# SSD decay sums through DRAM: a store and broadcast loads in place of ones-matmuls, and the head matmuls in one chain

## The chip, the core and the metric

One NeuronCore of a Trainium2 chip runs the whole program: TensorE (PE, with its weight loads shown as PEld), VectorE (DVE), ScalarE (ACT), GpSimd (POOL), SyncE (SP, which only issues transfers) and 16 DMA engines behind the queues of SP, ACT and POOL. The metric is device time in microseconds for one execution, the median of the runs shown. All arithmetic is float32; where a projection needs speed, an operand is split into a high and a low part in the faster format fp32r.

## What is computed

Two layers of a decoder over 256 positions and 2048 features. The change lies in layer 0, in its SSD mixer (32 heads of 64 channels, four groups of state size 128, one chunk of 256 positions):

```python
z, xbc, dt, q, k, v, gate = split(x @ w_in)
xs, bm, cm = split(silu(causal_depthwise_conv(xbc)))
dt = softplus(dt + dt_bias);  a = dt * -exp(a_log)      # per position and head
a_cum = cumsum(a)                                       # along the 256 positions
decay[l, s] = exp(a_cum[l] - a_cum[s])  for s <= l, else 0
y[l] = sum_s (cm[l] . bm[s]) * decay[l, s] * dt[s] * xs[s]  +  d_skip * xs[l]
y_a = rms_norm(y * silu(z))
```

Beside it, on the same input, runs an attention branch with 16 heads (q, k, v, gate). Both outputs go through one projection, a residual and a LayerNorm, and then layer 1 follows (a diagonal state-space mixer), which the change does not touch.

## The kernel before

The big projections set the frame. Each weight matrix comes in **units** of 512 KB: `split_to` loads one on SP's queue into a tile `raw` (four buffers), ACT copies it to a high part `wh`, and DVE subtracts to a low part `wl` (four buffers each). TensorE multiplies a unit while the next three are being prepared: `xmm` (L293) has 12 matmuls of 512 columns for a unit, and `product_wide` (L348, L349) 16 for a unit. So TensorE always has projection matmuls, and everything else is fitted in between.

That everything else is written as small **jobs**. After each unit, `pump` takes some of two queues: `jobs`, which has to be done by the end of the running projection, and `back`, which is spread evenly up to the unit `goal`. `run` puts the instructions of a job behind the load and the split of the unit two ahead, on each engine's queue. Beyond that, a scheduler that simulates the program in time orders each engine's instructions at build: among the ready ones it prefers those that were written earlier. `tc.issue_after(ins)` adds one rule to it: what is written inside and runs on the engine of `ins` is queued behind `ins`; it is an order, not a wait.

For SSD, `dt_jobs` computes dt and the cumulative sums for all 32 heads with heads on partitions: `r`, [32, 256]. `turn` (L559) transposes them into `dts` and `cums`, with positions on partitions, so that each position s has its scalar. The decay also needs the sums along the free axis, the same row on all 128 partitions. For that, `r` is split into a high and a low part in `cumhl` (L556, L557, rows 0 to 31 and 32 to 63, rest zero), and `sel` holds a unit vector for each head.

`head_jobs(k)` handles the two heads 2k and 2k+1, for k from 0 to 15, in steps:

- `bcast` (L842): for each head a matmul with one column of `sel` repeated 128 times as weights and `cumhl` as moving operand. It leaves the head's sums on all partitions in a PSUM tile of the pool `aux`.
- `decay` (L848 to L850): ACT computes relu(cums - row) for two halves of each head, out of PSUM into the tile `df` (tag b3, four buffers, shared with the rotary and attention tiles), then exp of the negative.
- `weigh` (L855 to L860): DVE multiplies with dt and the masked products of B and C (`cbm`), and adds the skip weight on the diagonal.
- `apply` (L872, L873): the product with the head's channels. A head's output has 64 rows, so head i of a pair writes partitions 64 i to 64 i + 63 and uses half of the array's columns. Its first matmul has 256 columns, its second 128, summed in PSUM; each float32 matmul shows as two records. An even and an odd k share one PSUM tile, and their applies are due in one step: a **couple** of four heads, eight couples in all.
- `comb` (L877 to L881): gate, square and sum, for the couple.

`skewed` lays these steps over one another: in background step t, apply belongs to k = t - 3 (and t - 4), weigh to t - 2, decay to t - 1, bcast to t. There are 20 steps; `goal` gives them the 48 units of the rest of the z projection and of q, k and v of the first attention group. The rotary jobs of q and k, which also use b3, run during the last 16 of these units.

Of the kernel before, what the change touches and what calls it, by code (L numbers as in the profile page):

```python
# [9 lines left out]
F32 = mybir.dt.float32  # L10
F32R = mybir.dt.float32r
AF = mybir.ActivationFunctionType
OP = mybir.AluOpType
# [3 lines left out]
P = 128  # L17
S = 256
# [3 lines left out]
CU = KT // UK  # L22
# [148 lines left out]
def trunk(tc, io, out):  # L171
# [8 lines left out]
    with ExitStack() as top:  # L180
# [10 lines left out]
        def C(name):  # L191
            lo, hi = CONST[name]
            return ct[:, lo:hi]

        def PR(name):
            lo, hi = PARAM[name]
            return pt[:, lo:hi]
# [3 lines left out]
        def aux():  # L201
            return auxp.tile([P, 512], F32, tag="aux", name=nm("aux"))
# [252 lines left out]
        with ExitStack() as l0:  # L455
# [6 lines left out]
            def b3(shape):  # L462
                return wk.tile(shape, F32, tag="b3", bufs=4, name=nm("b3"))
# [40 lines left out]
                    T.matmul(pdt, wdp[:, k, :], xh[:, k, :], start=k == 0, stop=False, skip_group_check=True)  # L504
                    T.matmul(pdt[:32], wdp[:, k, 0:32], xl[:, k, :], start=False, stop=k == KT - 1, skip_group_check=True)

            cumhl = wk.tile([P, S], F32R, name="cumhl")
            sel = cst.tile([P, 32], F32R, name="sel")
            G.memset(cumhl[64:128, :].bitcast(F32), 0.0)
            dts = wk.tile([P, 2, 32], F32, name="dts")  # L510
            cums = wk.tile([P, 2, 32], F32, name="cums")

            def dt_jobs():
                h = {}

                def soft1():
                    A.activation(sel, C("sel"), AF.Copy)
                    dw = wk.tile([32, 4, S], F32, tag="a4", bufs=6, name="dw")
                    ew = wk.tile([32, 4, S], F32, tag="a4", bufs=6, name="ew")
                    h["d"] = [dw[:, i, :] for i in range(4)]  # L520
                    h["e"] = [ew[:, i, :] for i in range(4)]
                    sx, na, e, r = h["d"]
                    A.activation(na, hdt["p"][32:64, :], AF.Copy)
                    V.scalar_tensor_tensor(sx, hdt["p"][0:32, :], PR("dtb")[:32, :], na, op0=OP.add, op1=OP.add)
                    V.scalar_tensor_tensor(na, sx, -1.0, sx, op0=OP.mult, op1=OP.min)
                    A.activation(e, na, AF.Exp)
                    V.tensor_scalar(r, e, 2.0, None, op0=OP.add)
                    V.reciprocal(r, r)

                def soft2():  # L530
                    sx, na, e, r = h["d"]
                    u, w2, pl, dtv = h["e"]
                    G.tensor_tensor(u, e, r, op=OP.mult)
                    G.tensor_tensor(w2, u, u, op=OP.mult)
                    G.tensor_scalar(pl, w2, 1.0 / 17, None, op0=OP.mult)
                    for k in range(7, 4, -1):
                        G.tensor_scalar(pl, pl, 1.0 / (2 * k + 1), None, op0=OP.add)
                        G.tensor_tensor(pl, pl, w2, op=OP.mult)

                def soft3():  # L540
                    u, w2, pl, dtv = h["e"]
                    for k in range(4, -1, -1):
                        G.tensor_scalar(pl, pl, 1.0 / (2 * k + 1), None, op0=OP.add)
                        G.tensor_tensor(pl, pl, w2 if k else u, op=OP.mult)

                def soft4():
                    sx, na, e, r = h["d"]
                    u, w2, pl, dtv = h["e"]
                    V.tensor_scalar(sx, sx, 0.0, None, op0=OP.max)
                    V.scalar_tensor_tensor(dtv, pl, 2.0, sx, op0=OP.mult, op1=OP.add)  # L550
                    ea = wk.tile([32, 1], F32, name="ea")
                    A.activation(ea, PR("alog")[:32, :], AF.Exp)
                    V.tensor_scalar(na, dtv, ea, -1.0, op0=OP.mult, op1=OP.mult)
                    V.memset(e, 1.0)
                    V.tensor_tensor_scan(r, e, na, 0.0, op0=OP.mult, op1=OP.add)
                    A.activation(cumhl[0:32, :], r, AF.Copy)  # L556
                    V.tensor_tensor(cumhl[32:64, :], r, cumhl[0:32, :].bitcast(F32), op=OP.subtract)  # L557

                def turn():  # L559
                    sx, na, e, r = h["d"]  # L560
                    u, w2, pl, dtv = h["e"]
                    px = aux()
                    for t in range(2):
                        T.transpose(px[:, t * 32 : t * 32 + 32], dtv[:, t * P : t * P + P], ident[:32, :32])
                        T.transpose(px[:, 64 + t * 32 : 96 + t * 32], r[:, t * P : t * P + P], ident[:32, :32])
                    A.activation(dts.rearrange("p t h -> p (t h)"), px[:, 0:64], AF.Copy)
                    A.activation(cums.rearrange("p t h -> p (t h)"), px[:, 64:128], AF.Copy)

                return [soft1, soft2, soft3, soft4, turn]
# [261 lines left out]
            G.memset(ssq, 0.0)  # L831
            G.memset(ones, 1.0)

            def head_jobs(k):
                d = {}
                g = k // 4
                heads = [(i, 2 * k + i) for i in range(2)]

                def bcast():
                    d["px"] = aux()  # L840
                    for i, h in heads:
                        T.matmul(d["px"][:, i * 256 : i * 256 + 256], sel[:, h : h + 1].to_broadcast([P, P]), cumhl, start=True, stop=True)  # L842

                def decay():
                    df = d["df"] = b3([P, 2, 384])
                    for i, h in heads:
                        pc = d["px"][:, i * 256 : i * 256 + 256]
                        A.activation(df[:, i, 0:256], pc, AF.Relu, bias=cums[:, 0, h : h + 1], scale=-1.0)  # L848
                        A.activation(df[:, i, 256:384], pc[:, 128:256], AF.Relu, bias=cums[:, 1, h : h + 1], scale=-1.0)
                    A.activation(df, df, AF.Exp, scale=-1.0)  # L850

                def weigh():
                    df = d["df"]
                    for i, h in heads:
                        V.scalar_tensor_tensor(df[:, i, 0:256], df[:, i, 0:256], dts[:, 0, h : h + 1], cbm[:, g, 0:256],  # L855
                                               op0=OP.mult, op1=OP.mult)
                        V.scalar_tensor_tensor(df[:, i, 256:384], df[:, i, 256:384], dts[:, 1, h : h + 1], cbm[:, g, 256:384],
                                               op0=OP.mult, op1=OP.mult)
                        dg = df[:, i, :].rearrange("p (b n) -> p b n", b=3)[:, 0:3:2, :]
                        V.scalar_tensor_tensor(dg, ident.unsqueeze(1).to_broadcast([P, 2, P]), PR("ssdd")[:, h : h + 1], dg,  # L860
                                               op0=OP.mult, op1=OP.add)

                def apply():
                    if k % 2 == 0:
                        pairy[0] = aux()
                    y = d["y"] = pairy[0]
                    df = d["df"]
                    yp = y[:, (k % 2) * S : (k % 2) * S + S]
                    for i, h in heads:
                        xc = slice(64 * h, 64 * h + 64)  # L870
                        yo = yp[64 * i : 64 * i + 64, :]
                        T.matmul(yo, xs[:, 0, xc], df[:, i, 0:256], start=True, stop=False)  # L872
                        T.matmul(yo[:, 128:256], xs[:, 1, xc], df[:, i, 256:384], start=False, stop=True)  # L873

                def comb():
                    sv = sz[:, k - 1 : k + 1, :].rearrange("p f n -> p (f n)")
                    V.tensor_tensor(sv, d["y"], sv, op=OP.mult)  # L877
                    jk = c2([P, 2, S])
                    A.activation(jk.rearrange("p f n -> p (f n)"), sv, AF.Square)  # L879
                    for f in range(2):  # L880
                        G.tensor_tensor(ssq, ssq, jk[:, f, :], op=OP.add)  # L881

                return [bcast, decay, weigh, apply, comb] if k % 2 else [bcast, decay, weigh, lambda: None, apply]

            pairy = [None]

            def skewed(lists):
                n = max(len(x) for x in lists)
# [19 lines left out]
            for j in range(4):  # L908
                zs = sz[:, 4 * j : 4 * j + 4, :]
                product_wide(xhl, lambda zs=zs: zs, lambda h, zs=zs: jobs.append(lambda: A.activation(zs, zs, AF.Silu)) if h else None)  # L910
                if j == 0:
                    jobs.extend(held)
                    goal[0] = unit[0] + 6 * CU
                    back.extend(skewed([head_jobs(k) for k in range(16)]))

            yb = {}
# [618 lines left out]
```

## Time and profile before

| | us |
|---|---|
| median of 3 runs | 1332.26 |
| lowest, highest | 1331.92, 1332.73 |
| profiled execution, its own time | 1332.87 |
| its span, first to last instruction | 1331.0 |
| mean granted TensorE clock | 0.999 |

The profile gives each engine's busy time, the chain of work that ended last, and groups of instructions by line with what ended the idle time before them. A line such as `L842 PE MATMUL aux<-cumhl,sel 128*128 128x256 f32 x32 | 7.4, 307 | 0.0` reads: line 842, engine, operation, what it writes and reads, its form, the count, then busy us, mean ns of one, and idle us before. Matmuls overlap, so their lengths do not add up; the order in time has start and length of each in microseconds from the start of the span.

### The profile page before, as it was taken

How to read it: one execution, taken by the hardware profiler on the slowest of the kernel's cores; microseconds unless marked ns; L12 is line 12 of the kernel's file. 1: busy time of each engine (PE TensorE's matmuls, PEld its weight loads, DVE VectorE, ACT ScalarE, POOL GpSimd, SP SyncE). 2: the span in 40 equal slices, each digit the busy share in tenths (PEclk: the TensorE clock that was granted, in tenths of full speed). 3: DMA queues.
4: the chain of work that ended last, by engine and by line, in shares of the span. 5: the costliest groups of instructions: out<-in, count | busy, mean ns of one | idle time of the engine just before them, and what ended most of it. 6: DMA issues, size and time to landing. Idle time of an engine off the chain costs nothing.

```text
span 1331.0 us, 21530 instructions
## 1 busy us (share of the span) xinstructions
PE 1321.8 (99%) x8079; PEld 1111.5 (84%) x8079; DVE 961.6 (72%) x1612; ACT 692.8 (52%) x947; POOL 337.9 (25%) x646
## 2 busy tenths in 40 slices
PE   9999999999999999999999999999999999999998
PEld 8988888877888888888888888888888888888886
DVE  6778877775686777687797765858999846555565
ACT  5556668864644554554564434443445544444442
POOL 0043000121036625334787300023453100000000
PEclk9999999999999999999999999999999999999999
DMA  8555555444556657656757768469998675555762
GB/s 318 175 183 181 180 175 174 155 149 157 173 190 225 196 204 234 201 189 202 235 189 247 253 230 308 173 232 308 321 292 303 216 215 188 190 190 190 252 211 90
DMA packets 80732, 282.73 MB, mean 212 GB/s; under 512 B 9842, under 2 KB 12658, under 8 KB 80116
## 3 DMA queue, kind: packets, MB, share of 16 engines
q1 hardware_dynamic: 68260, 239.64, 54.4%
q0 software_dynamic: 7328, 30.42, 6.8%
q10 hardware_dynamic: 5040, 11.31, 2.4%
q8 instruction: 63, 1.03, 0.3%
q14 instruction: 41, 0.34, 0.1%
HBM read 260.35 MB, written 20.97 MB: 211 GB/s over the span
## 4 chain that ended last, share of the span: by engine, by line
PE 97%; DMA 2%; DVE 0%; ACT 0%; issue 0%; SPq 0%; ACTq 0%; POOLq 0%
PE main L293 61%; PE main L348 16%; PE main L349 8%; PE main L315 3%; PE aux L429 2%; DMA ud<-ut 1%; PE aux L872 1%; PE aux L780 1%; DMA um<-ud 1%; PE dec L1335 1%; PE aux L961 1%; PE enc L1290 1%; PE aux L993 1%; PE dec L1331 0%; PE aux L790 0%; PE aux L842 0%
## 5 line engine op out<-in xcount | busy, mean ns | idle before, releaser
L249 DVE TENSOR_TENSOR wl<-raw,wh 128x1024 fp32r<-128x1024 f32 x430 | 533.1, 1242 | 306.5 <-ACT wh L244 304.4
L244 ACT ACTIVATE wh<-raw 128x1024 fp32r<-128x1024 f32 x430 | 455.2, 1060 | 518.4 <-PE main L293 313.4
L293 PE MATMUL main<-wh,A 128*128 128x512 f32 x1536 | 490.0, 394 | 0.0
L293 PEld LDWEIGHTS main<-wh,A 128*128 128x128 f32 x1536 | 287.8, 188 | 59.2 <-issue 0.3
L293 PE MATMUL main<-wl,A 128*128 128x512 f32 x768 | 300.7, 392 | 0.0
L348 PE MATMUL main<-A,wh 128*128 128x512 f32 x768 | 273.1, 399 | 0.0
L293 PE MATMUL main<-wh,C 128*128 128x512 f32 x832 | 262.4, 393 | 0.3 <-ACT C L1110 0.3
L349 PE MATMUL main<-A,wl 128*128 128x256 f32 x768 | 215.3, 280 | 0.0
L293 PEld LDWEIGHTS main<-wh,C 128*128 128x128 f32 x832 | 155.6, 188 | 34.0 <-ACT C L1110 1.0
L348 PEld LDWEIGHTS main<-A,wh 128*128 128x128 f32 x768 | 144.2, 188 | 33.6
L293 PEld LDWEIGHTS main<-wl,A 128*128 128x128 f32 x768 | 144.3, 188 | 29.2 <-issue 0.5
L293 PE MATMUL main<-wl,C 128*128 128x512 f32 x416 | 162.5, 391 | 0.0
L349 PEld LDWEIGHTS main<-A,wl 128*128 128x128 f32 x768 | 145.1, 189 | 0.2
L706 POOL TENSOR_TENSOR c<-c 128x8 f32<-128x8 f32 (+2 forms) x192 | 97.3, 525 | 28.6 <-DMA wb<-c 21.0
L293 PEld LDWEIGHTS main<-wl,C 128*128 128x128 f32 x416 | 78.1, 188 | 16.2
L348 PE MATMUL main<-C,wh 128*128 128x512 f32 x192 | 68.2, 399 | 0.0
L934 POOL TENSOR_TENSOR b<-b 128x128 f32<-128x128 f32 x16 | 11.4, 710 | 194.5 <-DVE b L933 151.6
L881 POOL TENSOR_TENSOR ssq<-ssq,c 128x256 f32<-128x256 f32 x16 | 18.4, 1147 | 166.4 <-ACT c L879 165.9
L349 PE MATMUL main<-C,wl 128*128 128x256 f32 x192 | 53.6, 281 | 0.0
L708 POOL TENSOR_TENSOR c<-c,c 128x4 f32<-128x4 f32 (+2 forms) x96 | 46.5, 485 | 7.4
L709 POOL TENSOR_TENSOR c<-c,c 128x4 f32<-128x4 f32 (+2 forms) x96 | 45.7, 476 | 0.0
L315 PE MATMUL main<-A,wh 128*128 128x256 f32 x256 | 43.4, 284 | 1.4 <-ACT wh L236 1.4
(302 smaller groups left out, 1379.2 us busy)
## 6 DMA issues: line engine op xcount, KB each, us to landing
raw<-in_wi SPq DMA_DIRECT2D x270, 512.0 KB, 3.7
raw<-in_wo SPq DMA_DIRECT2D x96, 512.0 KB, 4.3
raw<-in_wglu SPq DMA_DIRECT2D x64, 512.0 KB, 3.3
wt<-wb POOLq DMA_DIRECT2D x16, 896.0 KB, 7.4
wb<-ob ACTq DMA_DIRECT2D x16, 512.0 KB, 5.1
bc<-in_s5bc SPq DMA_DIRECT2D x16, 256.0 KB, 3.8
wb<-c POOLq DMA_DIRECT2D x16, 256.0 KB, 3.8
wb<-om ACTq DMA_DIRECT2D x16, 128.0 KB, 3.3
```

What stands on the lines that cost most here:

```text
L244: high = A.activation(wh, raw, AF.Copy)
L249: splits[n] = (loaded[-1], high, V.tensor_tensor(wl, raw, wh.bitcast(F32), op=OP.subtract))
L293: end = T.matmul(ps[o], l[:, k, sl], r[:, j, :], start=start and i == 0, stop=stop and i == 2)
L315: T.matmul(pv[o // 2][:, o % 2, :], l[:, j, sl], r[:, k, :], start=first and i == 0 and o % 2 == 0, stop=end and i == 2 and o % 2 == 1, sk ...
L348: T.matmul(ps[o], wh[:, j, sl], xx[:, k, :, :].rearrange("p a n -> p (a n)"), start=first, stop=False, skip_group_check=True)
L349: T.matmul(ps[o][:, S : 2 * S], wl[:, j, sl], xh[:, k, :], start=False, stop=end, skip_group_check=True)
L429: end = T.transpose(dst[:, i * P : i * P + P], s, ident)
L706: G.tensor_tensor(p[:, :, :, 0:m], cs[:, :, :, 1 : m + 1], cs[:, i, :, n : n + 1].unsqueeze(1).to_broadcast([P, 2, 4, m]), op=OP.mult)
L708: G.tensor_tensor(cs[:, 0, :, n + 1 : n + 1 + m], p0[:, 0, :, 0:m], p1[:, 1, :, 0:m], op=OP.subtract)
L709: G.tensor_tensor(cs[:, 1, :, n + 1 : n + 1 + m], p0[:, 1, :, 0:m], p1[:, 0, :, 0:m], op=OP.add)
L780: T.matmul(pk[at : at + 64, 64 * n + a * 16 : 64 * n + a * 16 + 16], d["ev"][:, a, 64 * i : 64 * i + 64], cv[:, a, i, :], start=True, stop ...
L881: G.tensor_tensor(ssq, ssq, jk[:, f, :], op=OP.add)
```

## The change

The cumulative sums `r` are written to a tile `cumd` in DRAM by a DMA on POOL's queue, in place of the high and low parts; `cumhl`, `sel` and their filling are gone. A new first step `spread` takes the place of `bcast`: it allocates `df` and loads the two heads' rows on SP's queue into it, each repeated over all 128 partitions. `decay` reads them there and works in place, the second half first. `apply` is now one function of the odd k, for both k of the couple: it gives out the four heads' matmuls in turns (odd k first), each queued behind the one before. `goal` becomes three units smaller.

```diff
-            cumhl = wk.tile([P, S], F32R, name="cumhl")
-            sel = cst.tile([P, 32], F32R, name="sel")
-            G.memset(cumhl[64:128, :].bitcast(F32), 0.0)
+            cumd = dram.tile([32, S], F32, name="cumd")
...
-                    A.activation(sel, C("sel"), AF.Copy)
...
-                    A.activation(cumhl[0:32, :], r, AF.Copy)
-                    V.tensor_tensor(cumhl[32:64, :], r, cumhl[0:32, :].bitcast(F32), op=OP.subtract)
+                    nc.gpsimd.dma_start(cumd, r)
...
+            couple = {}
+
             def head_jobs(k):
-                d = {}
+                d = couple[k % 2] = {}
+                pair = (couple.get(0), d)
...
-                def bcast():
-                    d["px"] = aux()
+                def spread():
+                    d["df"] = b3([P, 2, 384])
+                    nc.sync.dma_start(d["df"][:, :, 0:256], cumd.rearrange("(k i) n -> k i n", i=2)[k : k + 1].to_broadcast([P, 2, S]))
+
+                def decay():
+                    df = d["df"]
                     for i, h in heads:
-                        T.matmul(d["px"][:, i * 256 : i * 256 + 256], sel[:, h : h + 1].to_broadcast([P, P]), cumhl, start=True, stop=True)
-
-                def decay():
-                    df = d["df"] = b3([P, 2, 384])
-                    for i, h in heads:
-                        pc = d["px"][:, i * 256 : i * 256 + 256]
-                        A.activation(df[:, i, 0:256], pc, AF.Relu, bias=cums[:, 0, h : h + 1], scale=-1.0)
-                        A.activation(df[:, i, 256:384], pc[:, 128:256], AF.Relu, bias=cums[:, 1, h : h + 1], scale=-1.0)
+                        A.activation(df[:, i, 256:384], df[:, i, 128:256], AF.Relu, bias=cums[:, 1, h : h + 1], scale=-1.0)
+                        A.activation(df[:, i, 0:256], df[:, i, 0:256], AF.Relu, bias=cums[:, 0, h : h + 1], scale=-1.0)
                     A.activation(df, df, AF.Exp, scale=-1.0)
...
-                        V.scalar_tensor_tensor(dg, ident.unsqueeze(1).to_broadcast([P, 2, P]), PR("ssdd")[:, h : h + 1], dg,
-                                               op0=OP.mult, op1=OP.add)
+                        d["w"] = V.scalar_tensor_tensor(dg, ident.unsqueeze(1).to_broadcast([P, 2, P]), PR("ssdd")[:, h : h + 1], dg,
+                                                        op0=OP.mult, op1=OP.add)

                 def apply():
-                    if k % 2 == 0:
-                        pairy[0] = aux()
-                    y = d["y"] = pairy[0]
-                    df = d["df"]
-                    yp = y[:, (k % 2) * S : (k % 2) * S + S]
-                    for i, h in heads:
-                        xc = slice(64 * h, 64 * h + 64)
-                        yo = yp[64 * i : 64 * i + 64, :]
-                        T.matmul(yo, xs[:, 0, xc], df[:, i, 0:256], start=True, stop=False)
-                        T.matmul(yo[:, 128:256], xs[:, 1, xc], df[:, i, 256:384], start=False, stop=True)
+                    y = d["y"] = aux()
+                    ahead = d["w"]
+                    for n, e in ((1, pair[1]), (0, pair[0])):
+                        for part in range(2):
+                            for i in range(2):
+                                h = 2 * (k - 1 + n) + i
+                                yo = y[64 * i : 64 * i + 64, n * S : n * S + S]
+                                xc = slice(64 * h, 64 * h + 64)
+                                with tc.issue_after(ahead.ins):
+                                    if part:
+                                        ahead = T.matmul(yo[:, 128:256], xs[:, 1, xc], e["df"][:, i, 256:384], start=False, stop=True)
+                                    else:
+                                        ahead = T.matmul(yo, xs[:, 0, xc], e["df"][:, i, 0:256], start=True, stop=False)
...
-                return [bcast, decay, weigh, apply, comb] if k % 2 else [bcast, decay, weigh, lambda: None, apply]
-
-            pairy = [None]
+                return [spread, decay, weigh, apply, comb] if k % 2 else [spread, decay, weigh]
...
-                    goal[0] = unit[0] + 6 * CU
+                    goal[0] = unit[0] + 6 * CU - 3
```

## The prediction

> **What bounds the kernel now.** I read the page first, then the busy time of the stretch in which the changed work lies, then single instructions of TensorE in order of time, then the groups and the waits of the engines that feed it.
>
> ```profile
> span 1331.0 us, 21530 instructions
> ...
> PE 1321.8 (99%) x8079; PEld 1111.5 (84%) x8079; DVE 961.6 (72%) x1612; ACT 692.8 (52%) x947; POOL 337.9 (25%) x646
> ...
> PE 97%; DMA 2%; DVE 0%; ACT 0%; issue 0%; SPq 0%; ACTq 0%; POOLq 0%
> ```
>
> ```profile
> 184.00:330.00 146.00, 146.00 (x802) 119.92 (x801) 103.27 (x172) 102.95 (x164) 21.50 (x20) 1.00 0.49 159
> ```
>
> TensorE is busy 99% of the span and is 97% of the chain that ended last. The second view gives, for 184 to 330 us, busy time of PE, PEld, DVE, ACT and POOL, then clock, DMA share and GB/s. All broadcasts and applies lie in there, and PE has no hole: 146.00 of 146.00 us. So in this stretch a matmul costs what it pushes the next projection matmul back, and an edit on another engine costs nothing as long as the weight splits that PE needs stay ahead.
>
> **How a matmul is priced.** Since matmuls overlap, I use the distance from start to start. A lone broadcast, and the couple of heads k = 6, 7 with one behind it (columns: start, length, engine, line, operation, tiles, form, count; one float32 matmul is two records):
>
> ```profile
> 263.57 0.39 PE L293 MATMUL main<-wh,A 128*128 128x512 f32 x1
> 263.79 0.40 PE L842 MATMUL aux<-cumhl,sel 128*128 128x256 f32 x2
> 264.03 0.40 PE L293 MATMUL main<-wh,A 128*128 128x512 f32 x1
> 264.26 0.40 PE L293 MATMUL main<-wl,A 128*128 128x512 f32 x1
> ```
>
> ```profile
> 256.19 0.39 PE L293 MATMUL main<-wh,A 128*128 128x512 f32 x1
> 256.50 0.66 PE L872 MATMUL aux<-b,C 128*64 128x256 f32 x4
> 256.99 0.40 PE L873 MATMUL aux<-b,C 128*64 128x128 f32 x4
> 257.20 0.65 PE L872 MATMUL aux<-b,C 128*64 128x256 f32 x4
> ...
> 258.01 0.50 PE L842 MATMUL aux<-cumhl,sel 128*128 128x256 f32 x2
> 258.34 0.40 PE L293 MATMUL main<-wh,A 128*128 128x512 f32 x1
> 258.58 0.39 PE L293 MATMUL main<-wl,A 128*128 128x512 f32 x1
> ```
>
> A projection step is 264.26 - 264.03 = 0.23 us. From 263.57 to 264.03 are 0.46, so the two broadcast matmuls of one k cost 0.46 - 0.23 = **0.23 us**. For a couple I count from the projection matmul before it to the second one after it, less one step for each projection matmul in between: 258.58 - 256.19 - 2 x 0.23 = 1.93, broadcast included. Couple k = 12, 13 has none:
>
> ```profile
> 301.00 0.40 PE L293 MATMUL main<-wh,A 128*128 128x512 f32 x1
> 302.83 0.50 PE L293 MATMUL main<-wh,A 128*128 128x512 f32 x1
> 303.17 0.39 PE L293 MATMUL main<-wl,A 128*128 128x512 f32 x1
> ```
>
> 303.17 - 301.00 - 0.46 = **1.71 us** for four heads given out whole; 1.93 - 1.71 = 0.22 confirms the broadcast. In the rows of k = 6, 7 two heads (four records of L872, four of L873) take 257.20 - 256.50 = 0.70.
>
> **Part 1, broadcasts leave TensorE.** The group of L842 in that stretch:
>
> ```profile
> L842 PE MATMUL aux<-cumhl,sel 128*128 128x256 f32 x32 | 7.4, 307 | 0.0
> ```
>
> 32 matmuls, two for each of 16 k: 16 x 0.23 = **3.7 us** off the path. [...] With them go three small operations that fill cumhl and sel, before this stretch and not on PE; nothing for them.
>
> **Part 2, the applies in one chain.** Which of the eight couples are not whole today? I went through all; k = 8, 9, then 10, 11, then 14, 15:
>
> ```profile
> 269.29 0.39 PE L293 MATMUL main<-wh,A 128*128 128x512 f32 x1
> 272.38 0.39 PE L293 MATMUL main<-wh,A 128*128 128x512 f32 x1
> 272.61 0.40 PE L293 MATMUL main<-wl,A 128*128 128x512 f32 x1
> ```
>
> ```profile
> 286.06 0.39 PE L293 MATMUL main<-wh,A 128*128 128x512 f32 x1
> 288.16 0.40 PE L293 MATMUL main<-wh,A 128*128 128x512 f32 x1
> 288.49 0.65 PE L872 MATMUL aux<-b,C 128*64 128x256 f32 x2
> 288.98 0.38 PE L873 MATMUL aux<-b,C 128*64 128x128 f32 x2
> 289.29 0.50 PE L293 MATMUL main<-wl,A 128*128 128x512 f32 x1
> 289.62 0.40 PE L293 MATMUL main<-wh,A 128*128 128x512 f32 x1
> ```
>
> ```profile
> 316.34 0.39 PE L293 MATMUL main<-wh,A 128*128 128x512 f32 x1
> 317.46 0.50 PE L293 MATMUL main<-wh,A 128*128 128x512 f32 x1
> 318.69 0.50 PE L293 MATMUL main<-wl,A 128*128 128x512 f32 x1
> 319.03 0.63 PE L293 MATMUL main<-wh,A 128*128 128x512 f32 x2
> 320.38 0.50 PE L293 MATMUL main<-wl,A 128*128 128x512 f32 x1
> 320.71 0.40 PE L293 MATMUL main<-wh,A 128*128 128x512 f32 x1
> ```
>
> The first: 3.32 - 0.46 - 0.23 (its broadcast) = 2.63. The second, three steps in between: 3.56 - 0.69 - 0.23 = 2.64. The third, six steps (one row holds two) and no broadcast: 4.37 - 1.38 = 2.99. Over 1.71 that is 0.92 + 0.93 + 1.28 = **3.1 us**, the most that Part 2 can save. The other five are whole, and the new order of a whole couple is the one that they show, two heads side by side, so nothing is saved there.
>
> Will the new chain be whole? Its first link is the first head of the odd k, and what it is told to stand behind is a VectorE instruction; that orders VectorE's queue alone. So this link may go as soon as its own head is weighed, while the second, the other head of the odd k, may still be unweighed; projection matmuls then come in between. The price of such a break, from the lone head at 288.49: getting in 288.49 - 288.16 - 0.23 = 0.10, its two L872 records 0.49, getting out 0.31 less 0.21 for the L873 part (256.99 to 257.20) = 0.10, and the slow step behind it 0.33 - 0.23 = 0.10: **0.8 us** for each couple broken. Bounds: none broken (0) to all eight (6.4). The three late couples of today are the likely ones. Spreading the 20 background steps over the units by the rule of pump, the weigh of the odd k and the apply come two units apart in six of eight couples now, and in seven with 45 units in place of 48 (three in the rest), so lateness does not go away. In k = 8, 9 only the broadcast of k = 12 lies between the last two heads, so the delay there is near nothing. I take two broken, -1.6.
>
> **Part 3, the spreads.** One 32 KB store on POOL's queue, two products ahead of the first reader, and 16 loads of 256 KB on SP's. The rows closest to these, and the feeding of PE in the same stretch:
>
> ```profile
> raw<-in_wi SPq DMA_DIRECT2D x270, 512.0 KB, 3.7
> ...
> bc<-in_s5bc SPq DMA_DIRECT2D x16, 256.0 KB, 3.8
> ...
> row<-in_lnr SPq DMA_DIRECT2D x2, 1024.0 KB, 6.7
> ```
>
> ```profile
> L249 DVE TENSOR_TENSOR wl<-raw,wh 128x1024 fp32r<-128x1024 f32 x44 | 56.1, 1275 | 42.0 <-ACT wh L244 42.0
> L244 ACT ACTIVATE wh<-raw 128x1024 fp32r<-128x1024 f32 x45 | 47.6, 1058 | 39.7 <-PE main L293 23.9 <-PE main L348 11.2 <-issue 4.3
> ```
>
> ```profile
> SPq L723 <- DVE tm L762: 5.3, 7, 1.7
> ```
>
> The row broadcast lands 1024 KB over all partitions in 6.7 us, bc 256 KB in 3.8; I take 3.8 for a spread. A background step comes every 2.25 units, a unit being 12 steps = 2.75 us, so decay follows 6.2 us after its spread. 16 x 256 KB = 4.2 MB over 146 us are 29 GB/s on top of 159, at a DMA share of 0.49. ACT waits 35.1 us of this stretch for PE to free a split buffer, so the splits run as far ahead as their four buffers let them: a split that starts when PE ends unit n is wanted three units later, 8.25 us, and takes 1.06 + 1.28 = 2.3. That slack of 6 us hides both the spreads and any change of ACT's Relu (it now reads SBUF in place; I take 0). If it were gone, each late microsecond would be one of PE's.
>
> **The sum.** 3.7 + 3.1 - 1.6 = **5.2 us**. The profiled execution took 1332.87 us, its span 1331.0 and 1.9 around it; 1332.87 - 5.2 = 1327.7. The median shown is 0.6 below the profiled execution, so on the median 1332.26 - 5.2 = **1327.0**.
>
> **Rivals.** (a) The chain is whole everywhere: gain 6.8, 1325.4. For it: five of eight are whole today; against: the first link's freedom. (b) The chain saves nothing, since late heads cost what they cost before: only the broadcasts, 1328.5; the change then does half of what it says. (c) All eight break after the first link: 6.8 - 6.4 = 0.4, 1331.8. Against: five couples' heads were all ready today.
>
> (d) **Slower: a spread holds SP's queue.** With four buffers, the spread of an even k takes the buffer of k - 4, whose last reader is the apply in the same step. If it stands in SP's queue ahead of the load for unit n + 4, that load goes only after the run behind unit n. It lands 3.7 later, or 3.8 + 3.7 = 7.5 if it also waits for the spread's landing; with the split's 2.3 that is 6.0 to 9.8 against 8.25: 0 to 1.6 us late, for the six even k from 4 to 14, up to 9.6: 1336.6. It decides from 5.2 / 6 = 0.9 us each. Against: the bc loads also wait in that queue for a buffer, and stood there 1.7 us at most. [...]
>
> (e) **Slower: the links are torn apart**, each given out alone between projection matmuls. A first half alone is 0.8, a second 0.21 + 0.30 = 0.5: 4 x 1.3 = 5.2 for a couple, 3.5 over a whole one, 28 in all, less 6.8: 21 us slower, 1353. It decides from two couples on. Against: a head's second half follows its first without a projection matmul in between in the rows at 288.49 and 288.98, although it too has to come behind the first.
>
> **How the numbers follow.** Forecast (one to four couples broken, gain 3.6 to 6.0) 38%; (a) 28%; (b) 12%; (c) 8%; (d) 9%, of which 2 stay within the bound; (e) 5%. A measurement of this kernel can tell about 0.2%, 2.7 us, from no change. Faster: 38 + 28 + 12 = 78%; same: 8 + 2 = 10%; slower 7 + 5 = 12%. The range goes from 0.6 under (a), the distance of the profiled execution from the median, 1324.8, to (c), 1331.8; what is left out is (d), (e) and a little below. The likeliest case alone spans 1326.3 to 1328.7.
>
> **What would show it.** No L842 group on PE, PE still without a hole from 184 to 325 us, and that stretch 5 us shorter for the same projection matmuls. Runs of 16 records of L872/L873's successors at 1.71 us: right on Part 2; two records alone, then projection matmuls: the break of 0.8. Loads that SP issues only after an apply, and splits of ACT waiting for a DMA: (d). Wrong would be PE waiting for a split, or a saving outside this stretch.

## The result, and the profile after

The changed kernel takes 1325.97 us (median of 4 runs, 1324.77 to 1326.99) against 1332.49 us before (4 runs, 1331.92 to 1333.31): 6.5 us less, a ratio of 0.995 with a 95% interval of 0.9938 to 0.9963. The profiled execution took 1325.9 us, 1324.1 of them the span (1331.0 before). Two runs below stand far outside all others, one of the kernel before at 3397.35 us and one of the kernel without turns at 1821.96, and the ratios leave them out; their cause is not known. The page of the kernel after, its span, its busy times and the shares of the chain that ended last:

```profile
span 1324.1 us, 21499 instructions
...
PE 1315.2 (99%) x8047; PEld 1106.4 (84%) x8047; DVE 959.7 (72%) x1611; ACT 694.7 (52%) x945; POOL 340.2 (26%) x646
...
PE 99%; DMA 0%; ACT 0%; DVE 0%; issue 0%; SPq 0%; ACTq 0%
```

PE has 32 instructions less: 8079 - 8047, the broadcasts. It is still the whole chain. The window over the same 146 us as in the prediction (PE, PEld, DVE, ACT, POOL, then clock, DMA share, GB/s) has no hole in PE either; what it has more of is transfers, 195 GB/s instead of 159:

```profile
184.00:330.00 146.00, 146.00 (x802) 119.86 (x802) 105.82 (x175) 107.46 (x168) 21.94 (x20) 1.00 0.58 195
```

Now the couples, in TensorE's instructions in order of time (start, length, engine, line, operation, tiles, form, count). L873 is now the first, L871 the second part of a head. First k = 2, 3, which stands for the seven whole ones (four heads with no projection matmul in between), then k = 0, 1, the only one that is not whole:

```profile
222.35 0.28 PE L349 MATMUL main<-A,wl 128*128 128x256 f32 x1
...
222.70 0.28 PE L349 MATMUL main<-A,wl 128*128 128x256 f32 x1
222.91 0.65 PE L873 MATMUL aux<-b,C 128*64 128x256 f32 x4
223.39 0.39 PE L871 MATMUL aux<-b,C 128*64 128x128 f32 x4
223.61 0.60 PE L873 MATMUL aux<-b,C 128*64 128x256 f32 x4
224.04 0.39 PE L871 MATMUL aux<-b,C 128*64 128x128 f32 x4
224.36 0.50 PE L348 MATMUL main<-A,wh 128*128 128x512 f32 x1
224.70 0.28 PE L349 MATMUL main<-A,wl 128*128 128x256 f32 x1
```

```profile
206.41 0.28 PE L349 MATMUL main<-A,wl 128*128 128x256 f32 x1
206.62 0.65 PE L873 MATMUL aux<-b,C 128*64 128x256 f32 x2
207.20 0.50 PE L348 MATMUL main<-A,wh 128*128 128x512 f32 x1
...
208.32 0.43 PE L873 MATMUL aux<-b,C 128*64 128x256 f32 x1
...
209.76 0.38 PE L349 MATMUL main<-A,wl 128*128 128x256 f32 x1
...
210.22 0.28 PE L349 MATMUL main<-A,wl 128*128 128x256 f32 x1
```

A pair of L348 and L349 takes 222.70 - 222.35 = 0.35 us here. The whole couple costs 224.70 - 222.70 - 0.35 = **1.65 us**. In the other, four such pairs lie between 206.41 and 210.22 (four of their matmuls, from 207.53 to 208.00, are in rows left out), so it costs 3.81 - 4 x 0.35 = **2.41 us**: the first link went alone, five projection matmuls came behind it, and the break cost 2.41 - 1.65 = 0.76. It stands so in the program's order of TensorE instructions already:

```
1095 L349 Matmult main_2166<-A_73,wl_2143 128x256
1096 L873 Matmult aux_2247<-b_265_2080,C_683 64x256
1097 L348 Matmult main_2165<-A_73,wh_2169 128x512
...
1101 L348 Matmult main_2165<-A_73,wh_2169 128x512
1102 L873 Matmult aux_2247<-b_265_2080,C_683 64x256
```

Counted in this way, start to start over every broadcast and apply, these matmuls push the projections back by 20.8 us before and by 14.1 after: 6.7 us, of the 6.9 that the spans differ by. Comparing the start of the same projection matmul in both traces, the changed kernel is 0.3 us ahead at 100 us, 0.8 at 184, just before the first broadcast, 0.7 at 208, 4.0 at 277, 7.2 at 350, and from there to the end between 7.0 and 7.2. So 6.4 us come out of the stretch that was changed, and nothing of it is given back later.

The 0.8 from before that stretch is not explained by the change's sum. Of it, 0.3 arises in the first 10 us; the traces of the experiments below have 0.3 to 0.8 there. The other 0.5 comes from the projection pairs themselves: seventeen pairs take 133.81 - 127.80 = 6.01 us in the kernel before and 133.73 - 127.83 = 5.90 in the changed one, and in other stretches it is the other way round. This 0.5 is in the traces of all kernels below that have the spreads, and not in that of the chain alone, so it seems to come with them; what sets the pace of the pairs is not known, and it blurs every account here by some tenths of a microsecond.

The spreads are in the trace as follows: the group of their DMAs (tiles, queue, count, KB each, median us to landing), SP's waits between 184 and 330 us (what waited, for what: total, times, longest), and some of SP's queue in order of time:

```profile
b<-cumd SPq DMA_DIRECT2D x16, 256.0 KB, 3.7
```

```profile
SPq L241 <- DVE wl L249: 105.1, 42, 5.4
...
SPq L840 <- PE aux L871: 7.6, 10, 1.5
```

```profile
223.82 1.03 SPq L840 DMA_DIRECT2D b<-cumd  x2
225.65 11.43 SPq L241 DMA_DIRECT2D raw<-in_wi  x4
238.54 1.03 SPq L840 DMA_DIRECT2D b<-cumd  x2
```

A spread (L840) does wait for the apply that frees its buffer, but never over 1.5 us, because the weight loads (L241) stand ahead of it in the queue: four or five of them between one pair of spreads and the next. When a spread is at the head, its buffer is nearly free.

### The profile page after: what moved, and what is told of

It is laid out like the page before. It is cut to its first block, busy times and chain, and to the rows that moved or that the text cites. A ratio compares the mean times of both kernels' runs of the same rounds, so it can differ in the third digit from the quotient of the medians.

```text
span 1324.1 us, 21499 instructions
## 1 busy us (share of the span) xinstructions
PE 1315.2 (99%) x8047; PEld 1106.4 (84%) x8047; DVE 959.7 (72%) x1611; ACT 694.7 (52%) x945; POOL 340.2 (26%) x646
## 4 chain that ended last, share of the span: by engine, by line
PE 99%; DMA 0%; ACT 0%; DVE 0%; issue 0%; SPq 0%; ACTq 0%
PE main L293 61%; PE main L348 17%; PE main L349 9%; PE main L315 3%; PE aux L429 2%; PE aux L873 1%; PE enc L1288 1%; PE aux L776 1%; PE dec L1333 1%; PE aux L959 1%; PE aux L991 1%; PE dec L1329 0%; PE aux L786 0%; DMA raw<-in_wi 0%; PE turn L429 0%; PE aux L871 0%
## 5 line engine op out<-in xcount | busy, mean ns | idle before, releaser
L348 PE MATMUL main<-A,wh 128*128 128x512 f32 x768 | 273.2, 400 | 0.0
L349 PE MATMUL main<-A,wl 128*128 128x256 f32 x768 | 215.3, 280 | 0.0
L348 PEld LDWEIGHTS main<-A,wh 128*128 128x128 f32 x768 | 144.2, 188 | 34.7 <-ACT b L846 0.4
L349 PEld LDWEIGHTS main<-A,wl 128*128 128x128 f32 x768 | 145.0, 189 | 0.4 <-issue 0.2
L702 POOL TENSOR_TENSOR c<-c 128x8 f32<-128x8 f32 (+2 forms) x192 | 100.8, 543 | 27.4 <-DMA wb<-c 19.8
L348 PE MATMUL main<-C,wh 128*128 128x512 f32 x192 | 68.4, 400 | 0.0
L349 PE MATMUL main<-C,wl 128*128 128x256 f32 x192 | 53.6, 282 | 0.0
L705 POOL TENSOR_TENSOR c<-c,c 128x4 f32<-128x4 f32 (+2 forms) x96 | 45.6, 475 | 0.0
L704 POOL TENSOR_TENSOR c<-c,c 128x4 f32<-128x4 f32 (+2 forms) x96 | 41.7, 434 | 7.4
```

The costliest lines, as they stand in the source:

```text
L348: T.matmul(ps[o], wh[:, j, sl], xx[:, k, :, :].rearrange("p a n -> p (a n)"), start=first, stop=False, skip_group_check=True)
L349: T.matmul(ps[o][:, S : 2 * S], wl[:, j, sl], xh[:, k, :], start=False, stop=end, skip_group_check=True)
L702: G.tensor_tensor(p[:, :, :, 0:m], cs[:, :, :, 1 : m + 1], cs[:, i, :, n : n + 1].unsqueeze(1).to_broadcast([P, 2, 4, m]), op=OP.mult)
L704: G.tensor_tensor(cs[:, 0, :, n + 1 : n + 1 + m], p0[:, 0, :, 0:m], p1[:, 1, :, 0:m], op=OP.subtract)
L705: G.tensor_tensor(cs[:, 1, :, n + 1 : n + 1 + m], p0[:, 1, :, 0:m], p1[:, 0, :, 0:m], op=OP.add)
```

## The experiments

Ten kernels; each is timed beside runs of the kernel before (medians 1332.60, 1332.54 and 1333.56 us in the three sets), and ratios are to these.

**One part at a time.** First the spreads alone, with the applies as before and 48 units:

```diff
                 def apply():
-                    y = d["y"] = aux()
-                    ahead = d["w"]
...
+                    if k % 2 == 0:
+                        pairy[0] = aux()
+                    y = d["y"] = pairy[0]
...
-                return [spread, decay, weigh, apply, comb] if k % 2 else [spread, decay, weigh]
+                return [spread, decay, weigh, apply, comb] if k % 2 else [spread, decay, weigh, lambda: None, apply]
...
-                    goal[0] = unit[0] + 6 * CU - 3
+                    goal[0] = unit[0] + 6 * CU
```

> Only Part 1: the spreads replace the broadcasts, the applies stay as they were, two heads after two, and the background has 48 units. Theory (TensorE's own time decides, by starts): 16 x 0.23 = 3.7 us less, plus what the new order in time happens to do to late heads; in the order given out three couples are not whole (k = 10, 11, then 12, 13, then 14, 15), with about 2.1 us over whole couples against 3.1 before, so 3.7 + 1.0 = 4.7: about 1327.8 where before is 1332.5. Rival 1 (the chain does nearly all of it): less than 2 us saved. Rival 2 (broadcasts cost their busy time): 7.4 us saved, 1325.

1328.48 us (1328.28 to 1328.89), ratio 0.9966 (0.9954 to 0.9979): 4.1 less. Broadcasts and applies together push the projections back by 16.6 us instead of 20.8. Three couples are late, as many as before: k = 10, 11, then 12, 13, then 14, 15, with 3.01, 2.04 and 3.01 us, against 1.70 for the five whole ones. Here the first of them:

```profile
281.69 0.66 PE L869 MATMUL aux<-b,C 128*64 128x256 f32 x4
...
282.50 0.50 PE L293 MATMUL main<-wh,A 128*128 128x512 f32 x1
282.93 0.65 PE L869 MATMUL aux<-b,C 128*64 128x256 f32 x2
...
284.62 0.65 PE L869 MATMUL aux<-b,C 128*64 128x256 f32 x2
```

The heads come in three portions, with projection matmuls in between. The late couples take 8.06 us together, where those of the kernel before take 8.30; the expectation had counted on 1.0 less. Of the 4.2 us that the rows save, some 3.9 are thus the broadcasts', near the 3.7 foreseen, and the late heads are not their doing.

Then the chain alone, made from the kernel before: broadcasts stay, and apply and `goal` are as in the change.

```diff
+            couple = {}
...
-                d = {}
+                d = couple[k % 2] = {}
+                pair = (couple.get(0), d)
...
-                return [bcast, decay, weigh, apply, comb] if k % 2 else [bcast, decay, weigh, lambda: None, apply]
+                return [bcast, decay, weigh, apply, comb] if k % 2 else [bcast, decay, weigh]
...
-                    goal[0] = unit[0] + 6 * CU
+                    goal[0] = unit[0] + 6 * CU - 3
```

> Only Part 2: the broadcasts stay, the applies come in one chain and in turns, 45 units. In the order given out, four couples break after the first link. Theory (a whole couple 1.65, a break 0.8): 3.1 + 8 x 0.06 - 4 x 0.8 = 0.4 us saved, about 1332.1. Rival (the chain by itself is the larger part of the 6.5): 3 us or more saved, 1329.5 or less.

1331.99 us (1331.45 to 1333.97), ratio 0.9997 (0.9988 to 1.0006): 0.6 less, not to be told from nothing. Four of eight couples are broken after their first link, here k = 6, 7:

```profile
250.72 0.65 PE L879 MATMUL aux<-b,C 128*64 128x256 f32 x2
251.29 0.50 PE L845 MATMUL aux<-cumhl,sel 128*128 128x256 f32 x2
251.63 0.40 PE L293 MATMUL main<-wh,A 128*128 128x512 f32 x1
```

Such a break costs about 1.0 us with the 0.23 of the broadcast that comes behind it, so 0.8, and the rest of the couple costs 1.65. The chain gathers the late heads and gives the gain back in breaks. The two parts together (6.5) are worth more than their sum (4.1 + 0.6): with the spreads one couple breaks, without them four do. Why the heads stand closer to their applies with the spreads was not tried by itself.

**The first link.** The break needs a first link that is ready before the second. VectorE weighs head 0 of the odd k first and head 1 last. Here head 1 leads:

```diff
                         for part in range(2):
-                            for i in range(2):
+                            for i in (1, 0):
```

> The changed kernel, with the two heads of each pair in the other order, so that the first link is the head that is weighed last. Theory (a link given out before its partner is weighed breaks the chain, 0.8 us each): all eight couples whole, one break less than the changed kernel, 0.8 us faster than it: 1325.2 where before is 1332.5, eight couples of 1.65 us. Rival (the break costs nothing because projection matmuls fill the gap): same as the changed kernel, 1326.0.

1325.19 us (1324.51 to 1326.63), ratio 0.9941 (0.9928 to 0.9954). All eight couples are whole, 1.65 to 1.67 each; here k = 0, 1, the one that was broken:

```profile
207.41 0.39 PE L348 MATMUL main<-A,wh 128*128 128x512 f32 x1
207.73 0.65 PE L873 MATMUL aux<-b,C 128*64 128x256 f32 x4
...
209.41 0.39 PE L348 MATMUL main<-A,wh 128*128 128x512 f32 x1
```

209.41 - 207.41 - 0.35 = 1.65. The median is 0.78 below the changed kernel's, the price of the break; the runs of the two overlap, so the rows carry this more than the times.

The number of units was the other suspect. First the change with 48 units in place of 45, then the same with head 1 leading:

```diff
-                    goal[0] = unit[0] + 6 * CU - 3
+                    goal[0] = unit[0] + 6 * CU
```

> The changed kernel with the background spread over 48 units again instead of 45. In the order given out two couples break after the first link (k = 10, 11 and 12, 13) where the changed kernel has one (k = 0, 1). Theory (only whole and broken couples count, 0.8 us a break): 0.8 slower than the changed kernel, 1326.8 where before is 1332.6. Rival (the pace itself is worth something, because the last steps then come clear of the rotary jobs): 2 us slower or more, 1328.

> e3 with 48 units for the background instead of 45. All eight couples are whole in the order given out. Theory (only whole and broken couples count, the pace does not): as e3, 1325.2 where before is 1332.6. Rival (the smaller goal has a worth of its own): 1 us or more slower than e3.

With 48 units alone 1326.41 us (1326.14 to 1327.17), ratio 0.9954 (0.9942 to 0.9967), with two couples broken after the first link at 0.78 each. With head 1 leading as well 1325.11 us (1324.90 to 1325.71), ratio 0.9931 (0.9917 to 0.9946), and no break. The medians differ by 1.3, where two breaks are 1.55 by the rows; the two were timed in different sets and their intervals overlap, so here too the rows carry more than the times. With head 1 leading, 45 and 48 units cannot be told apart (1325.19 and 1325.11). Thus, in these four kernels, the pace only decides how many first links come too early. The two versions with head 1 leading have the lowest medians of all.

**The turns.** Does it matter that heads are given out in turns, part by part, and not one behind the other?

```diff
-                        for part in range(2):
-                            for i in range(2):
+                        for i in range(2):
+                            for part in range(2):
```

> The changed kernel with its chain head by head instead of in turns: both parts of a head, then both parts of the next. Theory 1 (TensorE pairs two heads on the two column halves by itself when they stand close in its queue): couples of 1.71 us in place of 1.65, about 0.5 us slower than the changed kernel, 1326.5. Theory 2 (only the turns put two heads side by side): four heads one after another, 0.70 us each, about 2.8 us a couple, 9 us slower than the changed kernel, 1335.

1326.46 us (1326.04 to 1326.62), ratio 0.9949 (0.9935 to 0.9963). Below, the program's order for k = 2, 3 and then what TensorE did:

```
1184 L873 Matmult aux_2403<-b_281_2201,C_683 64x256
1185 L871 Matmult aux_2403<-b_281_2201,C_683 64x128
1186 L873 Matmult aux_2403<-b_281_2201,C_683 64x256
1187 L871 Matmult aux_2403<-b_281_2201,C_683 64x128
```

```profile
223.16 0.28 PE L349 MATMUL main<-A,wl 128*128 128x256 f32 x1
223.37 0.66 PE L873 MATMUL aux<-b,C 128*64 128x256 f32 x4
223.85 0.40 PE L871 MATMUL aux<-b,C 128*64 128x128 f32 x4
...
225.21 0.28 PE L349 MATMUL main<-A,wl 128*128 128x256 f32 x1
```

The four records of the wide matmuls, two of each head, start ahead of any narrow one, although the second head's wide matmul is queued behind the first head's narrow one. TensorE pairs the two column halves by itself, at 225.21 - 223.16 - 0.35 = 1.70 us for a couple. The turns bring it to 1.65; what they are worth in all is 8 x 0.05 = 0.4 us. This rests on the rows: the medians differ by 0.5, and the runs of the two kernels overlap.

**The spreads' bytes, and their place.** Part 3 of the prediction put the spreads at nothing because of slack. Four kernels, all with head 1 leading, test that. In the first each spread is loaded a second time, into a tile that nobody reads:

```diff
+            twice = wk.tile([P, 2, S], F32, name="twice")
...
+                    nc.sync.dma_start(twice, rows)
```

> e3 with every spread loaded a second time, into a tile that nobody reads: 32 loads of 256 KB in place of 16, 4.2 MB more. Theory (transfers are hidden): as e3, 1325.2, within 0.5. Rival (the spreads' bytes slow the weight loads): 1 us or more slower.

1325.40 us (1325.25 to 1326.33), ratio 0.9947 (0.9934 to 0.9961): as without them. Another 4.2 MB cost nothing, so the bytes are hidden.

In the second no weight load may be queued on SP ahead of a spread that was given out before it, which is the order that rival (d) had in mind:

```diff
-                loaded.append(nc.sync.dma_start(raw.rearrange("p k n -> p (k n)"), units[n]))
+                with ExitStack() as pin:
+                    if spreads:
+                        pin.enter_context(tc.issue_after(spreads[-1].ins))
+                    loaded.append(nc.sync.dma_start(raw.rearrange("p k n -> p (k n)"), units[n]))
...
-                    nc.sync.dma_start(d["df"][:, :, 0:256], cumd.rearrange("(k i) n -> k i n", i=2)[k : k + 1].to_broadcast([P, 2, S]))
+                    spreads[:] = [nc.sync.dma_start(d["df"][:, :, 0:256], cumd.rearrange("(k i) n -> k i n", i=2)[k : k + 1].to_broadcast([P, 2, S]))]
```

> The changed kernel with the head order of e3 (all couples whole in the order given out), and every weight load queued on SP behind the last spread written before it, so that no load overtakes a spread that waits for its buffer. This is the worst order of the prediction's slower case. Theory (slack of 8.25 us against 3.7 for the load and 2.3 for the split hides it): as e3, 1325.2, PE without a hole. Rival (the hold costs up to 1.6 us for each of six spreads): up to 9.6 slower, 1330 to 1335, with PE waiting for splits and ACT for raw.

**1362.98 us** (1361.94 to 1363.91), ratio 1.0226 (1.0212 to 1.0240): 37.8 us more than the same kernel with the loads free, far above the theory and the rival alike. Its waits of SP from 180 to 360 us and, last, from 190 to 246 us, its waits of PE, and SP's queue for a while:

```profile
SPq L844 <- PE aux L875: 62.2, 6, 16.3
...
SPq L844 <- DVE b L861: 35.9, 3, 16.7
...
SPq L844 <- PE aux L875: 30.4, 3, 15.3
```

```profile
PE main L297 <- ACT wh L248: 17.9, 4, 6.4
PE main L352 <- ACT wh L248: 3.7, 1, 3.7
```

```profile
227.85 1.21 SPq L245 DMA_DIRECT2D raw<-in_wi  x2
244.37 0.38 SPq L844 DMA_DIRECT2D b<-cumd  x1
244.84 0.90 SPq L245 DMA_DIRECT2D raw<-in_wi  x2
245.79 0.42 SPq L844 DMA_DIRECT2D b<-cumd  x1
246.31 1.23 SPq L245 DMA_DIRECT2D raw<-in_wi  x2
```

The wait for an apply that was 1.5 us at most in the changed kernel (2.0 with head 1 leading) is now up to 16.3, and for the whole of it SP issues no load. Then two spreads and four loads go out within some three microseconds. The slack is used up, and PE stands still five times for 3.2 to 6.4 us, the first time until 251.4. The wait of 15.3 us ended at 244.3, before PE had stood at all: holds of this length come from the queue's order, in which SP reaches a spread long before the apply that frees its buffer, and not from PE's stops. How the stop at 247.7 goes on, by the windows of this kernel and PE's first matmul after it:

```profile
184.00:370.00 186.00, 162.60 (x812) 128.27 (x811) 107.59 (x177) 108.85 (x170) 20.37 (x20) 0.92 0.46 154
...
251.40:256.80 5.40, 5.35 (x16) 4.10 (x17) 5.24 (x8) 5.11 (x9) 0.32 (x1) 0.52 0.40 161
256.90:262.00 5.10, 5.10 (x25) 4.20 (x24) 5.10 (x11) 3.17 (x8) 1.56 (x2) 1.00 0.00 0
```

```profile
251.41 1.22 PE L352 MATMUL main<-A,wh 128*128 128x512 f32 x2 [3.69 <-ACT wh L248]
```

After 3.69 us without work the clock is 0.52 for 5.4 us, and these cost about 5.4 x 0.48 = 2.6 us more. So this late split is paid nearly twice. For the stretch from 184 to 370 us: 186 - 162.60 = 23.4 idle, and a mean clock of 0.92 gives up to 0.08 x 186 = 14.9; together 38.3, where the spans differ by 1362.1 - 1324.8 = 37.3.

The third goes further: two more loads of the same rows, nobody's to read, behind each spread, each waiting for the landing of the one before, and the weight loads behind them.

```diff
+                    spreads[:] = [nc.sync.dma_start(d["df"][:, :, 0:256], rows)]
+                    for n in range(2):
+                        with tc.issue_after(spreads[-1].ins):
+                            spreads[:] = [nc.sync.dma_start(more, rows)]
```

> e6 with two more loads of the same rows behind each spread, both into one tile, so that the second waits for the landing of the first, and the weight loads stand behind them: SP is held about 3.7 us more after each spread. Theory (slack as reckoned: 3.7 + 3.7 + 2.3 = 9.7 against 8.25, 1.4 late for each of the six spreads that wait for an apply): up to 9 us slower than e3, 1334; PE waits for splits of ACT and DVE, ACT for raw. Rival (the loads run further ahead than reckoned): as e3, 1325.2.

1388.66 us (1387.12 to 1389.98), ratio 1.0420 (1.0406 to 1.0434). SP's waits for these landings, from 180 to 400 us, come on top of those for the apply:

```profile
SPq L849 <- DMA more<-cumd: 78.6, 23, 4.7
```

Longer holds cost more: 63.5 us over the free loads, against 37.8, and again far more than the 9 that the theory allowed.

Was it the wait for the apply? In the last one the rows land in a tile of their own, which ACT's first step frees, so that no spread waits for TensorE's apply; the loads are behind the spreads as in the second.

```diff
-                    d["df"] = b3([P, 2, 384])
+                    d["row"] = wk.tile([P, 2, S], F32, tag="row", name=nm("row"))
...
-                        A.activation(df[:, i, 0:256], df[:, i, 0:256], AF.Relu, bias=cums[:, 0, h : h + 1], scale=-1.0)
+                        A.activation(df[:, i, 0:256], row[:, i, :], AF.Relu, bias=cums[:, 0, h : h + 1], scale=-1.0)
```

> e6 with one thing changed: a spread loads into a tile of its own (one buffer, free again when ACT's decay of the k before has read it), and df is taken only by decay. The order of SP's queue is that of e6, every weight load behind its spread; but a spread waits for ACT, which works on the splits three units ahead of TensorE, in place of an apply on TensorE. Theory (in e6 the wait for the apply's buffer at the head of SP's queue cost the 37 us, not the order and not the bytes): most of it gone, within 3 us of e3, 1325 to 1328. Rival (the order alone, loads behind 256 KB of spread and bursts of several transfers, costs it): near e6, above 1350.

1372.28 us (1371.88 to 1373.11), ratio 1.0283 (1.0265 to 1.0301): not better, but 8 to 9 us worse than with the wait for the apply (by the ratios and by the medians). SP's waits of this kernel, 180 to 380 us:

```profile
SPq L844 <- ACT b L851: 73.9, 12, 12.1
SPq L844 <- DMA row<-cumd: 45.4, 14, 3.8
```

The spread now waits for ACT's decay (L851), and ACT for its part waits 63.7 us of this stretch for weight loads, the very ones that SP holds; and, since there is one tile for all rows, for the spread before to land. So this kernel brings a wait of its own and does not acquit the apply's buffer. It shows that holds of another kind cost as much, and the theory that the apply's buffer alone is what costs falls. What the three kernels with a hold have in common is a wait at the head of SP's queue with weight loads behind it. How much of the price is the hold itself, and how much the crowd of transfers that land together after it, these runs do not separate.

## Why the prediction was right

The likeliest case came about: one to four couples broken. The time, 1325.97, is 1.0 below the predicted one and just below the 1326.3 at which that case was to begin, since a small saving was missed. By its steps:

- **What bounds the kernel: right.** PE had no hole in the stretch before and has none after, and 6.4 us of the gain stand in that stretch.
- **Part 1, the broadcasts: right.** 3.7 foreseen; the spreads alone gave 4.1, some 3.9 of it the broadcasts' by the rows.
- **Part 2, the three torn couples: right.** 3.1 foreseen; their rows before, counted with the same method, are 2.65, 2.64 and 3.01, and all three are whole after.
- **Part 2, the break: right in its place and its price, off in the count.** It was to come behind the first link and to cost 0.8; it does, at 0.76. Two were taken, one came, and in the chain alone four came. That it hangs on the first link is shown: with head 1 leading there is none at 45 units and none at 48.
- **Part 2, "the new order of a whole couple is the one that they show": wrong in a small term.** Before, the order was head by head, and the pairs that the rows showed were TensorE's doing. Giving the heads out in turns saves 0.05 to 0.06 of every couple, 0.4 in all. With one break less than foreseen this makes 3.7 + 3.1 + 0.4 - 0.8 = 6.4, where 6.5 was measured; that it fits to 0.1 is in part luck, since the pace of the projection pairs, which no term covers, had moved by half a microsecond before the stretch began.
- **Part 3, the spreads at nothing: the number was right, the reason was not.** It was argued from 6 us of slack. What keeps the spreads free is that loads are queued ahead of them; with loads behind them the slack did not hold. The working never read that order, so it was lucky here.
- **Rival (d): its mechanism exists, and its price was too small.** It was bounded by 0 to 1.6 us for each of six spreads, 9.6 in all. The order it needs was not the change's; forced, it cost 37.8. The working held one load until the apply and then added 3.7 or 7.5 for landing. That a load waits for the landing of the spread ahead of it, as the 7.5 has it, no run shows by itself; in the forced order two spreads and four loads went out together, and between 225 and 260 us the loads took 7.5 us to land and the spreads 6.8 (medians; 3.3 and 3.7 in the changed kernel from 184 to 330 us). In the runs SP stood up to 16.7 us at one spread, and already 15.3 before PE's first stop, several loads were late together, and the slow clock came on top (a mean of 0.92 over the stretch). None of these was in the sum. That each stop of PE also pushed the next apply back, and so held the next spread, fits the rows but was not tested.
- **The other rivals.** (a), all couples whole: 1325.4 foreseen, and the version that has it took 1325.19. (b) is out, since the chain does save with the spreads; (c) and (e) did not occur.

## What to carry to other kernels

Where TensorE has no idle time, price an edit in start-to-start distances of its own matmuls (here they gave 6.7 of the 6.9 us), and look for the early first link of any chain that is meant to run whole: let the operand that is ready last lead (the one break cost 0.76 us here). Here a transfer that waits for a buffer was harmless as long as the loads which feed the bound engine stood ahead of it in the queue, and cost 37.8 us when they stood behind it, so read the queue's order before trusting slack. When pricing a stop of TensorE, add the slow clock that followed it here: about 2.6 us behind a stop of 3.69.

## What was not expected of the hardware

TensorE started matmuls on the two column halves in another order than the one they were queued in: the second head's wide matmul ahead of the first head's narrow one, in the rows at 223.37 and 223.85 of the kernel without turns, where all four wide records start before any narrow one.

The clock of 0.52 after a stop of 3.69 us in the kernel with the loads behind the spreads, back to 1.00 some 5.4 us later, had no counterpart in the kernel before, whose PE never stood in this stretch. Shorter stops had a slow clock behind them too: in the kernel whose rows land in a tile of their own, TensorE stood 1.08 us, then 0.53, and the clock was 0.50 for the 3.3 us that follow:

```profile
299.81 0.73 PE L297 MATMUL main<-wh,A 128*128 128x512 f32 x2 [1.08 <-ACT wh L248]
301.07 0.64 PE L297 MATMUL main<-wl,A 128*128 128x512 f32 x1 [0.53 <-DVE wl L253]
```

```profile
301.30:304.60 3.30, 3.30 (x9) 2.53 (x9) 3.03 (x7) 1.89 (x4) 0.00 (x0) 0.50 0.33 47
```

How long a stop has to be for the clock to fall, these runs do not show.
